# Hybrid decoder trunk on one core: the order of the input projection's blocks

## The chip, the cores and the metric

The kernel runs on one core of one Trainium2 chip. The metric is device time in microseconds of the whole program, both layers, from one launch. Times are medians of a few runs on the chip. A trace of one profiled execution shows when each instruction ran on each engine: PE (TensorE, matmuls), PEld (its weight loads), DVE (VectorE), ACT (ScalarE), POOL (GpSimd) and SP (the queue that issues the DMAs).

## What is computed

The reference runs two layers on x of shape (1, 512, 1024). Each layer has a token mixer and a channel mixer, each between two RMSNorms and added to the residual stream. Cut to what matters here:

```python
proj = h @ w_in                                   # one input projection for both groups
a_qkv, a_z, a_b, a_a, b_q, b_k, b_v = split(proj)
# group a: gated delta rule, 4 heads of 128
a_qkv = silu(causal_dwconv(a_qkv, dn_conv))       # 4 taps
aq, ak, av = split(a_qkv); aq, ak = l2norm(aq), l2norm(ak)
beta = sigmoid(a_b); g = -exp(a_log) * softplus(a_a + dt_bias)
o_a = gated_delta_rule(aq, ak, av, g, beta)       # in chunks: invert a triangle made of k, g and beta,
                                                  # then a scan over chunks that takes v, k and q
o_a = rmsnorm(o_a) * silu(a_z)
# group b: attention, 8 heads of 64, three dilations merged into one masked softmax
o_b = dilated_attention(rope(b_q), rope(b_k), b_v)
out = concat(o_a, o_b) @ w_out
```

The channel mixer is `(gelu(gate) * val) @ ffn_down` over a causal 3-tap convolution of `h @ ffn_up`.

## The kernel before

The weights are a stream of units of 128 x 1024 floats. `loader` brings them by DMA into two buffers "raw"; `splitter` turns each into a pair of reduced-precision halves (`whi` on ACT, `wlo` on POOL or DVE), for which there are four places; a place comes free when the unit's products have been issued. Each product of the projection is three matmuls (hi x hi, hi x lo, lo x hi), called a triple below.

The input projection has seven blocks of four units each: the delta rule's k, v, q and z (gate), and the attention's bq, bk and bv. The tuple ORDER (line 35) sets both the order of the weight stream (line 226) and the order in which `mixer` computes the blocks (the loop `for name in ORDER` at its end). The first three units of k are computed ahead of that loop, by `lead`, while the residual rows are still being scaled.

Two kinds of block differ in what they need:

- k, v, q, z: one unit gives one head, a tile of 128 channels by 512 tokens, in one PSUM bank of the pool "psg", which has four. `conv` takes it out of the bank into a tile "A" (times 1/rms), after which the bank is free. There are two tiles "A". The convolution that follows is one ACT instruction and three DVE instructions (line 164), and only then is the tile "A" free. For z there is no convolution. `silu` runs once for all four heads of a block and loads ACT's table for silu and the one for exp again.
- bq, bk, bv: each unit holds two of the eight row blocks of the weight for all 512 columns, and each of the four token chunks has a bank of its own, so that all four banks of "psg" are in use until the fourth unit is done. The first unit goes chunk by chunk: `order = [(c, j) for c in range(NC) for j in range(2)]`, and a bank is asked for when its chunk begins. `rope` or `v_evac` then takes the banks out through ACT.

Beside the loop run jobs of the mixer: `gates` (beta, g, and their sums, many small DVE instructions), `decays` (tile edec), `k_head`, `inverse` (the 16 x 16 blocks row by row on DVE, by way of memory) and `doubles` (the inverse of each chunk's triangle, twice as large each time, many narrow matmuls), `v_head`, `q_head`, `qk`, `scan` (over four chunks; it needs v, the inverse, and from chunk 0's output on q), `merge`, `z_head`, and `attention`, which starts when bq, bk and bv are all there and goes through eight heads, each with four scores, softmax rows in tiles "A" and "B" (two each), transposes, and two products with v. `out_rows` then multiplies by w_out, its first three row tiles in whatever order the mixer's outputs come.

The order of the instructions on every engine is fixed when the program is built. `_Sched` (line 44) keeps a clock in TensorE time and an estimate of each engine's load; jobs are generators that yield the time at which they next have something to emit, and the job of highest priority that is due emits next. The mixer's loop over ORDER has the lowest priority, so its triples fill what the jobs leave. Each engine then runs its instructions in exactly that order, and waits where an operand is late.

Of the kernel before, what the change touches and what calls it, by code (L numbers as in the profile page):

```python
# [31 lines left out]
FULL = ((0, 512),)  # L32
CM = ("k", "v", "q", "z")
TM = ("bq", "bk", "bv")
ORDER = ("k", "v", "bq", "bk", "bv", "q", "z")

C_ID, C_U, C_M, C_COS, C_SIN, C_ONE, C_BD, C_EV, C_OD = 0, 128, 256, 512, 576, 640, 641, 655, 658
C_W = 664
# [3 lines left out]


class _Sched:
    """Orders the instructions of concurrent jobs by an estimate of when their operands are ready.

    A job is a generator that emits instructions and yields the time before which it has nothing to
    emit. Times are those of the tensor engine, which advances with the products emitted."""

    def __init__(self):  # L50
        self.t = 0.0
# [26 lines left out]
        return start + cost + 0.2  # L78

    def idle(self, engs, most):  # L80
        """The first of the engines that has nothing left to do, or, after a while, the one with least."""
        end = self.t + most
        while True:
            eng = min(engs, key=lambda e: self.free[e])
            if self.free[eng] <= self.t or self.t >= end:
                return eng
            yield min(self.free[eng], end)
# [25 lines left out]
def kernel(ctx: ExitStack, tc: tile.TileContext, xT, w_ab, w_cm, w_tm, w_o, w_up, w_dn,  # L113
# [13 lines left out]

    sc = _Sched()

# [1 line left out]
    def mm(ps, lhsT, rhs, start, stop):  # L131
        n = rhs.free_size()
        if rhs.dtype == F32R:
# [42 lines left out]
        nc.vector.reciprocal(out_, a)  # L176
        return sc.op("dve", 0.07 + out_.free_size() * 6.4e-3, after)

# [1 line left out]
    BUFS = {"A": 2, "B": 2, "C": 2, "sq": 2, "acc": 1, "acc2": 1, "vh": 1, "rs": 1}  # L180
    PB = {"g": 4, "s": 3, "o": 1}

# [26 lines left out]
    one = cc[:, C_ONE:C_ONE + 1]  # L209
# [10 lines left out]

    T_EXP, T_SILU, T_GELU = "exp_and_others", "silu_and_others", "gelu_apprx_tanh_and_others"

# [1 line left out]
    wseq = []  # L224
    for l in range(DEPTH):
        for name in ORDER:
# [65 lines left out]
        mm3(ps[:, t0:t1], hi[:, k * P:(k + 1) * P], lo[:, k * P:(k + 1) * P], xh[:, t0:t1], xl[:, t0:t1],  # L292
            first, last)

# [1 line left out]
    xt = [xp.tile([P, 2, S], F32, tag=f"x{j}", name=f"xt{j}") for j in range(4)]  # L296

    def xs(m):
# [33 lines left out]
    sc.set(("vec", 0))  # L332

    def row_rstd(acc, seg, dst, tok):
        """1/rms of the columns of seg, on every partition, from the sums of squares in acc."""
        t0, t1 = seg
        c0, c1 = t0 // P, t1 // P
        ps = yield from pget("o")
        for c in range(c0, c1):
            mm(ps[:, c:c + 1], acc[:, c * P:(c + 1) * P], one, True, True)  # L340
        r = ts(tok[:, c0:c1], ps[:, c0:c1], 1.0 / D, EPS, ALU.mult, ALU.add)
        yield r
        nc.gpsimd.tensor_tensor(tok[:, c0:c1], tok[:, c0:c1], mhalf[:, c0:c1], op=ALU.pow)
        r = sc.op("pool", 0.17 + 0.15 * (c1 - c0), r)
        yield r
        for c in range(c0, c1):
            mm(ps[:, c * P:(c + 1) * P], tok[:, c:c + 1].to_broadcast([P, P]), ident, True, True)
        r = act(dst[:, t0:t1], ps[:, t0:t1], AF.Copy)
        pput("o", r)
        return r  # L350
# [7 lines left out]
        return lambda kt: (tiles[kt][:, 0], tiles[kt][:, 1])  # L358

    def scale_split(key, m, seg, hx, gain, acc2, after):  # L360
        """x * gain as an exact pair, and x^2 added to acc2."""
        t0, t1 = seg
        x = xs(m)[:, t0:t1]
        hi = hx[m][:, 0, t0:t1]
        r = act(hi, x, AF.Identity, scale=gain, after=after)
        if key != "in":
            sc.spawn(square_sum(key, m, seg, acc2), 0)
        yield r
        r = stt(hx[m][:, 1, t0:t1], x, gain, hi.bitcast(F32), ALU.mult, ALU.subtract, after=r)
        sc.set(("hx", key, m, t0), r)  # L370
        if key == "in":
            yield from sc.idle(("act",), 6.0)
            yield from square_sum(key, m, seg, acc2)
# [21 lines left out]
        return sc.flags.get(flag, 1e9) <= sc.t  # L395

    def lead(key, pss, units, rhs, seg, last, extra=None):
        """The first row tiles of a product, in whatever order their operands come."""
        n = len(units)
        left = [(i, kt) for i in range(n) for kt in range(KD)]  # L400
        if extra is not None:
            left = left[:KD] + [(n, kt) for kt in range(KD)] + left[KD:]
        while left:
            for i, kt in left:
                if ready_at(("hx", key, kt, seg[0])) and (i == n or ready_at(("wu", units[i]))):
                    break
            else:
                yield sc.t + 0.1
                continue
            mine = [k for j, k in left if j == i]  # L410
            left.remove((i, kt))
            if i == n:
                extra(kt, seg, len(mine) == KD, len(mine) == 1)
            else:
                mmk(pss[i], wunit[units[i]], kt, rhs(kt), seg, len(mine) == KD, len(mine) == 1)
                if last and len(mine) == 1:
                    wunit.pop(units[i])
                    free()
            yield

    def out_rows(key, nt, rhs, nk, post, pre, dst, wait_rhs=None, flags=None):
        """The eight row tiles of a sub-layer's result, its norm, the residual sum and, for the next
        sub-layer, x * gain as an exact pair; the last row tile and what follows by halves of the tokens."""
        yield from sc.get("acc", 1)
        acc = work("acc")
        hw, sums = {}, []
# [27 lines left out]
        if flags is not None:  # L454
# [6 lines left out]
            left = list(range(nk))  # L461
# [32 lines left out]
        if pre is not None:  # L494
            yield from sc.get("acc2", 1)
            acc2 = work("acc2")
# [101 lines left out]
        sc.put("sq", r)  # L598
        return r

# [1 line left out]
    def next_ab(l):  # L602
        wa = load_ab(l)
        yield sc.t + 4.0
# [4 lines left out]
    def mixer(l, key, hx, acc2, rs, segs):  # L609
# [115 lines left out]
            sc.set(K("gates"), r)  # L725

        def conv(kind, h, ps, ptag):
            """Row tile of k, v, q (scaled, convolved) or z (scaled), before the silu."""
            yield from sc.wait(*ready)
            m = 4 * CM.index(kind) + h  # L730
            if kind == "z":
                yield from sc.wait(*[K("x", c) for c in range(NC)])
                if not zt:
                    zt.append(sp.tile([P, 4, S], F32, tag="s6", name="zt"))
                r = tt(zt[0][:, h], ps, rs, ALU.mult)
                pput(ptag, r)
            else:
                u = yield from wget("A")
                r = tt(u, ps, rs, ALU.mult)
                pput(ptag, r)  # L740
                yield r
                dst = {"k": kT, "v": vb, "q": qraw}[kind][:, h]
                y = dst.rearrange("p c t -> p (c t)") if kind == "v" else dst
                taps = [vv[:, V_DC + 4 * m + j:V_DC + 4 * m + j + 1] for j in range(4)]
                r = conv_first(y, u, taps, None, r)
                yield r
                r = conv_rest(y, u, taps, r)
                sc.put("A", r)
            sc.set(K("cv", kind, h), r)
# [116 lines left out]
            sc.put("acc", sc.t)  # L866

        def masked(c, lv):
            """The part that joins pairs of blocks, its columns those of the even blocks."""
            s = 16 << lv  # L870
            mask = cc[:, C_M + 64 * lv:C_M + 64 * (lv + 1)].rearrange("p (a k) -> p a k", k=s)
            return tt(xiT[:, c, :, 64 * lv:64 * (lv + 1)].rearrange("p h (a k) -> p h a k", k=s),
                      am[:, c].rearrange("p h (a b k) -> p h a b k", b=2, k=s)[:, :, :, 0],
                      mask.unsqueeze(1).to_broadcast([P, 4, 64 // s, s]), ALU.mult, eng="pool")

        def expand(dst, src, s, b0, eng="dve", after=0.0):
            """Rows of diagonal blocks of s columns, put in their places in a row of 128."""
            n, nb = dst.shape[0], dst.shape[2] // s
            return tt(dst.rearrange("p h (b k) -> p h b k", b=nb),
                      src.unsqueeze(2).to_broadcast([n, 4, nb, s]),  # L880
                      bc(cc[0:n, b0:b0 + nb], s).unsqueeze(1).to_broadcast([n, 4, nb, s]), ALU.mult, eng=eng,
                      after=after)

        def doubles(c, x):
            """The inverse of a chunk's triangle from those of its diagonal blocks, twice as large each time.

            A pair of blocks has the transposed inverse [[a, -a.t.b], [0, b]]; rows keep their block's columns
            only, and what the even blocks alone need is computed for these 64 rows."""
            tmp = yield from wget("C")
            lo, up = slice(0, 64), slice(64, P)  # L890

# [382 lines left out]
        return mixt  # L1274

    def reload(xd):
        """The residual rows come back from memory once nothing else uses their place."""
        yield from sc.wait(*[(lx[0], "mt", j) for j in range(KD)])
        for j in range(4):
            xt[j] = xp.tile([P, 2, S], F32, tag=f"x{j}", name=f"xt{j}")  # L1280
# [3 lines left out]
    HG = [None]  # L1284
    lx = [0]

# [1 line left out]
    def ffn(key, hx, acc2, rs):  # L1288
        rhs = hl(hx)
        hid = [None] * 11  # L1290
# [63 lines left out]

        return lambda kt: (hid[kt // 2][:, kt % 2, 0], hid[kt // 2][:, kt % 2, 1]), wait_hid

# [1 line left out]
    def trunk():  # L1358
        nonlocal vv, rc
        key = "in"  # L1360
# [140 lines left out]
```

## Time and profile before

| | us |
|---|---|
| median of 3 runs | 1469.94 |
| lowest and highest run | 1469.23, 1472.27 |
| span of the profiled execution | 1468.8 |
| both mixers' projections, attention and delta rule (39.85 to 295.60 and 762.75 to 1025.90) | 255.8 and 263.2 |

The page gives the span of the profiled execution from its first to its last instruction; the time around it isn't on the page, and the median of the timed runs lies 1.1 us above the span. Timeline rows give start, duration, engine, line, operation, what is written and read, shape, and a count where neighbours were merged; in brackets, how long the engine was idle before and what ended that. A row of a window table gives busy time and count of each engine, then the granted TensorE clock as a share of full speed, DMA share and GB/s.

### The profile page before, as it was taken

Reading aid. Unit: us, or ns where it says so; the run is one execution under the profiler, and the core shown is the slowest. Engines: PE = TensorE matmul, PEld = TensorE weight load, DVE = VectorE, ACT = ScalarE, POOL = GpSimd, SP = SyncE. Lnnn points to the kernel's source line nnn. Section 1 sums busy time; section 2 is a strip of 40 time slices with the busy share of each in tenths; the row PEclk is TensorE's granted clock in tenths of the full one; section 3 lists DMA queues with packets and bytes.
Section 4 is the critical chain, followed back from the end, with each engine's and each line's share of the span. In section 5 each row is a group of like instructions: output and inputs, shape, how many; then the busy total and the mean of one; then the engine's idle time right before and its main releaser. Section 6 shows DMA issues by size and latency. Waiting matters only on the chain.

```text
span 1468.8 us, 18826 instructions
## 1 busy us (share of the span) xinstructions
PE 1400.0 (95%) x7174; PEld 1155.5 (79%) x7174; DVE 941.8 (64%) x1497; ACT 610.3 (42%) x992; POOL 603.1 (41%) x365
## 2 busy tenths in 40 slices
PE   8999999998999999899999999999989999998996
PEld 5778766887888888788887877668878888887886
DVE  4885576757788877611479654668487887886113
ACT  4553456544543444322345423565255344433220
POOL 4244255315454444433343521553164444543332
PEclk9999999999999999999999987999989999999998
DMA  5233111041323322333232330110413332233331
GB/s 193 72 98 104 32 44 44 1 149 53 101 86 101 100 87 87 105 93 100 76 126 86 104 85 15 44 44 16 143 44 101 101 100 86 87 101 104 93 90 58
DMA packets 48698, 123.15 MB, mean 84 GB/s; under 512 B 15584, under 2 KB 18400, under 8 KB 48608
## 3 DMA queue, kind: packets, MB, share of 16 engines
q1 hardware_dynamic: 48608, 121.95, 26.7%
q8 instruction: 57, 0.93, 0.3%
q14 instruction: 33, 0.27, 0.1%
HBM read 115.11 MB, written 6.82 MB: 83 GB/s over the span
## 4 chain that ended last, share of the span: by engine, by line
PE 63%; DVE 25%; ACT 7%; issue 4%; DMA 0%; SPq 0%; POOL 0%; ACTq 0%; DVEq 0%
PE psg L137 49%; DVE B L164 12%; PE pss L137 9%; ACT B L146 3%; PE pso L137 2%; DVE kT L164 2%; DVE C L150 2%; ACT hid L146 1%; DVE xt L150 1%; PE pss L142 1%; DVE A L150 1%; PE psg L142 1%; DVE hx L164 1%; DVE zt L150 1%; ACT whi L146 1%
## 5 line engine op out<-in xcount | busy, mean ns | idle before, releaser
L137 PE MATMUL psg<-hx,whi 128*128 128x512 f32 (+1 forms) x2080 | 630.1, 386 | 0.9 <-DVE C L157 0.8
L150 POOL TENSOR_TENSOR wlo<-raw,whi 128x1024 fp32r<-128x1024 f32 (+1 forms) x159 | 394.5, 2490 | 557.9 <-ACT whi L146 535.8
L137 PEld LDWEIGHTS psg<-hx,whi 128*128 128x128 f32 x2080 | 378.8, 189 | 78.6 <-issue 4.9
L137 PE MATMUL psg<-hx,wlo 128*128 128x512 f32 (+1 forms) x1040 | 396.9, 382 | 0.0
L146 ACT ACTIVATE whi<-raw 128x1024 fp32r<-128x1024 f32 (+1 forms) x208 | 215.5, 1036 | 274.3 <-PE psg L137 212.5
L164 DVE SCALAR_TENSOR_TENSOR B<-A,vv,B 128x510 f32<-128x510 f32 (+1 forms) x176 | 275.3, 1565 | 76.9 <-ACT B L146 73.8
L137 PE MATMUL psg<-hid,whi 128*128 128x512 f32 (+1 forms) x792 | 224.8, 369 | 8.8 <-ACT hid L146 8.7
L137 PEld LDWEIGHTS psg<-hx,wlo 128*128 128x128 f32 x1040 | 196.6, 189 | 38.2
L137 PEld LDWEIGHTS psg<-hid,whi 128*128 128x128 f32 x792 | 144.5, 190 | 34.9 <-ACT hid L146 9.6
L137 PE MATMUL psg<-hid,wlo 128*128 128x512 f32 (+1 forms) x396 | 145.7, 368 | 0.0
L150 DVE TENSOR_TENSOR wlo<-raw,whi 128x1024 fp32r<-128x1024 f32 (+1 forms) x49 | 66.1, 1353 | 102.0 <-ACT whi L146 96.0
L137 PE MATMUL psg<-whi,hx 128*128 128x512 f32 x384 | 125.4, 408 | 0.3 <-DVE A L150 0.3
L146 ACT ACTIVATE hid<-C 128x512 fp32r<-128x512 f32 x44 | 27.7, 630 | 179.4 <-DVE C L150 179.4
L137 PE MATMUL pss<-hx,whi 128*128 128x256 f32 (+1 forms) x336 | 80.8, 330 | 20.9 <-DVE hx L164 18.5
L150 POOL TENSOR_TENSOR acc<-acc,sq 128x256 f32<-128x256 f32 (+1 forms) x65 | 67.7, 1041 | 75.1 <-ACT sq L146 72.0
L137 PEld LDWEIGHTS psg<-hid,wlo 128*128 128x128 f32 x396 | 75.3, 190 | 12.2
L137 PEld LDWEIGHTS pss<-hx,whi 128*128 128x128 f32 x336 | 61.0, 212 | 28.8 <-DVE hx L164 22.2
L146 ACT ACTIVATE B<-A,vv 128x512 f32<-128x512 f32 x88 | 71.0, 809 | 25.8 <-DVE A L150 24.5
L137 PEld LDWEIGHTS psg<-whi,hx 128*128 128x128 f32 x384 | 70.4, 192 | 13.7 <-DVE A L150 0.8
L137 PE MATMUL psg<-wlo,hx 128*128 128x512 f32 x192 | 76.4, 398 | 0.0
L150 DVE TENSOR_TENSOR A<-psg,rs 128x512 f32<-128x512 f32 x100 | 68.2, 684 | 2.0 <-POOL A L157 1.6
L137 PE MATMUL psg<-bT,bT 64*128 64x512 f32 (+3 forms) x128 | 48.4, 478 | 6.9 <-DVE nm L1151 4.2
(226 smaller groups left out, 1674.5 us busy)
## 6 DMA issues: line engine op xcount, KB each, us to landing
raw<-in_w_up_dram SPq DMA_DIRECT2D x88, 512.0 KB, 3.5
raw<-in_w_cm_dram SPq DMA_DIRECT2D x32, 512.0 KB, 3.6
raw<-in_w_dn_dram SPq DMA_DIRECT2D x32, 512.0 KB, 3.5
raw<-in_w_tm_dram SPq DMA_DIRECT2D x24, 512.0 KB, 3.5
raw<-in_w_o_dram SPq DMA_DIRECT2D x16, 512.0 KB, 3.6
raw<-in_w_dn_dram SPq DMA_DIRECT2D x16, 384.0 KB, 3.1
xt<-in_xT_dram SPq DMA_DIRECT2D x7, 512.0 KB, 6.9
scr_a<-am SPq DMA_DIRECT2D x8, 256.0 KB, 2.9
```

The costliest lines, as they stand in the source:

```text
L137: pe.matmul(ps, lhsT, rhs, start=start, stop=stop)
L142: pe.transpose(dst[:, i * P:(i + 1) * P], s, ident)
L146: nc.scalar.activation(out_, in_, func, **kw)
L150: (nc.vector if eng == "dve" else nc.gpsimd).tensor_tensor(out_, a, b, op=op)
L164: nc.vector.scalar_tensor_tensor(out_, a, s, b, op0=op0, op1=op1)
```

## The change

ORDER puts v behind the three attention blocks. Comments and docstrings were removed as well; the rest is the same code. The weight units are the same and are split in the same way, in the new order.

```diff
 CM = ("k", "v", "q", "z")
 TM = ("bq", "bk", "bv")
-ORDER = ("k", "v", "bq", "bk", "bv", "q", "z")
+ORDER = ("k", "bq", "bk", "bv", "v", "q", "z")
...
     for l in range(DEPTH):
         for name in ORDER:
...
         for name in ORDER:
             if name in CM:
```

## The prediction

> **What bounds the kernel now.** I read the page's first lines, then the busy time of each engine by stage, the list of TensorE's waits in the first mixer, and then the timelines of PE, DVE and POOL around the place where the order changes. First the page, with the rows of the weight loads from its list of DMA issues.
>
> ```profile
> span 1468.8 us, 18826 instructions
> PE 1400.0 (95%) x7174; PEld 1155.5 (79%) x7174; DVE 941.8 (64%) x1497; ACT 610.3 (42%) x992; POOL 603.1 (41%) x365
> ...
> raw<-in_w_cm_dram SPq DMA_DIRECT2D x32, 512.0 KB, 3.6
> ...
> raw<-in_w_tm_dram SPq DMA_DIRECT2D x24, 512.0 KB, 3.5
> ```
>
> PE is busy 95% of the span; no other engine is near it. The change alters no instruction and no count, only where the value units stand, so only time in which PE waits, or runs at a reduced clock, can change. The table by stage shows how much of that there is. In layer 0, 39.85 is where the last key unit ends and 165.70 where the attention projections end; 295.60 is where the output projection starts. In layer 1 the same places are 762.75, 896.27 and 1025.90; 145.40 and 866.20 are where the doubling of the inverse starts. Columns: stretch, PE, PEld, DVE, ACT, POOL (left out where it is zero), granted clock, DMA.
>
> ```profile
> 39.85:69.75 29.90, 27.46 (x141) 22.54 (x140) 25.93 (x47) 14.54 (x23) 9.84 (x4) 1.00 0.22 71
> ...
> 145.40:165.70 20.30, 19.95 (x166) 15.96 (x165) 8.73 (x28) 6.54 (x12) 2.40 (x1) 0.92 0.18 61
> 165.70:295.60 129.90, 123.32 (x713) 94.14 (x712) 91.03 (x239) 71.33 (x160) 59.27 (x42) 0.96 0.10 32
> ...
> 866.20:896.27 30.07, 28.81 (x167) 23.36 (x165) 9.71 (x28) 6.54 (x12) 2.36 (x1) 0.58 0.15 51
> 896.27:1025.90 129.63, 123.05 (x714) 94.06 (x712) 90.50 (x238) 71.64 (x160) 59.29 (x42) 0.97 0.11 33
> ```
>
> The stretch with attention, queries, gate and scan (165.70 to 295.60) already has PE busy 123.32 of 129.90 us: the query and gate units fill what attention leaves. Starting attention earlier therefore finds little idle PE time to fill. The 20.30 us of doubling in layer 0 take 30.07 us in layer 1, for the same work, at a clock of 0.58 instead of 0.92: 9.8 us that only the clock explains. The waits of PE between 33 and 296 us (total, times, longest), and behind them the first row of the same list for 755 to 1026 us:
>
> ```profile
> PE pso L137 <- DVE edec L150: 2.9, 2, 2.3
> PE psg L137 <- DVE nm L1151: 2.1, 1, 2.1
> PE pss L142 <- DVE kd L150: 1.7, 1, 1.7
> PE pso L137 <- DVE pt1l L150: 1.5, 1, 1.5
> PE psg L142 <- DVE pt L150: 1.4, 1, 1.4
> PE psg L137 <- DVE pt1l L150: 1.4, 1, 1.4
> ...
> PE psg L137 <- DVE A L150: 0.3, 1, 0.3
> ```
>
> ```profile
> PE pso L137 <- DVE edec L150: 3.0, 1, 3.0
> ```
>
> Two kinds: about 4.9 us early (edec, kd, A), while the key and value convolutions crowd DVE, and about 6.4 us in the attention stretch (nm, pt1l, pt). None names ACT.
>
> **The change part by part: the fourth bank.** A value, query or gate unit needs one PSUM bank of the pool "psg" (four banks). An attention projection needs all four at once: `pt` collects one per token chunk, and its first weight unit goes chunk by chunk, two row blocks each. Directly behind the keys, one bank is still held by the fourth key tile, k3, until its convolution takes it. The timelines of PE, DVE and POOL there:
>
> ```profile
> 39.62 0.39 PE L137 MATMUL psg<-hx,wlo 128*128 128x512 f32 x1
> 39.85 0.62 PE L137 MATMUL psg<-hx,whi 128*128 128x512 f32 x2
> ...
> 40.55 0.62 PE L137 MATMUL psg<-hx,whi 128*128 128x512 f32 x2
> ...
> 42.00 0.41 PE L668 MATMUL pso<-cc,C 16*128 16x16 f32 x4
> ...
> 57.05 0.39 PE L137 MATMUL psg<-hx,wlo 128*128 128x512 f32 x1
> 57.56 0.70 PE L137 MATMUL psg<-hx,whi 128*128 128x512 f32 x2
> ```
>
> ```profile
> 34.29 0.67 DVE L172 COPY C<-psg 16x512 f32<-16x512 f32 x1
> ...
> 47.10 8.83 DVE L164 SCALAR_TENSOR_TENSOR kT<-A,vv,kT 128x509 f32<-128x509 f32 x6
> 55.85 0.68 DVE L150 TENSOR_TENSOR A<-pss,rs 128x512 f32<-128x512 f32 x1
> ...
> 56.74 0.68 DVE L150 TENSOR_TENSOR A<-psg,rs 128x512 f32<-128x512 f32 x1
> 57.34 6.67 DVE L164 SCALAR_TENSOR_TENSOR kT<-A,vv,kT 128x509 f32<-128x509 f32 x6
> ...
> 68.08 4.55 DVE L164 SCALAR_TENSOR_TENSOR vb<-A,vv,vb 128x509 f32<-128x509 f32 x6 [0.34 <-ACT vb L146]
> ```
>
> ```profile
> 47.05 2.39 POOL L150 TENSOR_TENSOR wlo<-raw,whi 128x1024 fp32r<-128x1024 f32 x1 [3.70 <-ACT whi L146]
> 52.99 2.39 POOL L150 TENSOR_TENSOR wlo<-raw,whi 128x1024 fp32r<-128x1024 f32 x1 [3.55 <-DMA raw<-in_w_tm_dram]
> ```
>
> The small-gate bank is free from 34.96 (34.29 + 0.67). k3's is freed only at 57.42 (56.74 + 0.68): its evacuation needs a tile "A", of which there are two, and those are held by k0 and k1 until the six products from 47.10 are done. Before, three value units of about 5.6 us stood in that gap (8 triples of 0.70, from the starts 39.85 and 40.55), and the fourth starts at 57.56, right behind the evacuation; the bank was just not missed. After, PE does three chunks (six triples, 4.2 us, and the 0.41 us of L668) and stops at 44.4. The group from 47.10 ends at 47.10 + 8.83 = 55.93 today. DVE's gate chain up to 47.10 doesn't depend on the order. The six products then take 4.55 us, as the value ones at 68.08 did, not 8.83: the two POOL splits beside them cost the rest, (8.83 - 4.55)/2 = 2.1 each, and those weights are split later or earlier because no unit is freed meanwhile. So 51.7, and from there to k3's evacuation as before, 57.42 - 55.93 = 1.5: 53.2. PE waits from 44.4 to 53.2, less some 0.5 for the four g sums, which still go out in between: **8.2 us** (12.5 if the splits stay where they are; 4.4 if the key products go ahead of the gate chain).
>
> Layer 1, the same views:
>
> ```profile
> 762.75 0.62 PE L137 MATMUL psg<-hx,whi 128*128 128x512 f32 x2
> ```
>
> ```profile
> 766.46 8.71 DVE L164 SCALAR_TENSOR_TENSOR kT<-A,vv,kT 128x509 f32<-128x509 f32 x6
> ...
> 775.97 0.68 DVE L150 TENSOR_TENSOR A<-psg,rs 128x512 f32<-128x512 f32 x1
> ```
>
> Three chunks end at 762.75 + 4.2 = 766.9. One of two POOL splits remains, since its weights land late: 766.46 + 6.6 + 1.5 = 774.6. **7.2 us** after 0.5 for the g sums (5 to 9.4). Behind the blocked PE nothing else is queued that is ready: decays and key transposes need the key convolutions. The weight stream is 512 KB a unit at 3.5 to 3.6 us in either order, so SP's queue sees the same loads with two names exchanged.
>
> **The clock after the waits.** Rows in steps of 4 us around two waits of today, 2.1 us at 248 and 3.0 us at 782:
>
> ```profile
> 248.00:252.00 4.00, 1.89 (x3) 0.50 (x2) 3.50 (x8) 1.19 (x4) 4.00 (x3) 0.70 0.28 72
> 252.00:256.00 4.00, 4.00 (x14) 3.47 (x14) 0.83 (x4) 0.57 (x1) 2.79 (x3) 0.50 0.15 59
> ...
> 784.00:788.00 4.00, 2.91 (x15) 2.91 (x16) 2.14 (x4) 3.97 (x5) 0.00 (x0) 0.68 0.03 10
> 788.00:792.00 4.00, 4.00 (x24) 3.64 (x23) 3.86 (x7) 3.94 (x7) 0.00 (x0) 0.89 0.00 0
> ```
>
> The first loses 4 x (0.30 + 0.50) = 3.2 us of full clock, the second 4 x (0.32 + 0.11) = 1.7. For two waits I take 2 each, **+4** (0 to 6.4).
>
> **What the early crowd loses.** With the value convolutions gone from the first 40 us, DVE reaches the decays sooner. The early waits are 4.9 us in layer 0, and 3.0 and the 1.7 of clock in layer 1: 9.6. The key convolutions stay, so I take two thirds, **-6.4** (0 to -9.6).
>
> **What the values bring to attention.** Four value convolutions (4 x 2.3 us of DVE) and their silu now lie among softmax rows and doublings. The query convolutions do so today, beside waits of 1.4 us for pt and pt1l. I take 2 us a layer, **+4** (0, if the heads have slack, to 13, if both layers repeat the 2.1 + 1.4 us waits with a 3.2 us clock loss). The silu adds ACT time only, and no PE wait names ACT.
>
> **The doubling.** It moves beside attention and value units. In the old order its second half already runs beside the first heads. Layer 1, after 896.27:
>
> ```profile
> 900.00:916.00 16.00, 16.00 (x124) 11.38 (x124) 10.12 (x43) 7.74 (x23) 4.34 (x5) 1.00 0.11 34
> ```
>
> The clock is 1.00 there. I take the 9.8 us of layer 1 as gone, **-9.8** (0 to -9.8).
>
> **The end of the mixer.** Attention starts some 34 us earlier (the four value units, 22 us, and the 20.3 us of doubling no longer stand ahead of it, the 8.2 us wait does) and ends before the scan; queries stay sixth of seven, so the scan starts no earlier. The chain from queries to output projection is covered by the gate units (32 triples, 22 us), the scan's own products and the attention half of the output projection. I take 0 (-3 to +8).
>
> Sum: 8.2 + 7.2 + 4 - 6.4 + 4 - 9.8 = **+7.2 us** on the profiled execution (span 1468.8). The median lies 1.1 above that span, so I add the sum to it: 1469.9 + 7.2 = **1477 us**.
>
> **Rivals.** First, the clock stretch stays, in one layer or the other. For it: both layers ran the same doubling, and only one was throttled. Then +17.0: 1487. [...]
>
> Second, DVE becomes the bound while attention, doubling and eight convolutions lie together: 13 in place of 4, so +16: 1486. DVE is busy 91.03 of 129.90 in the attention stretch today, without doubling and values; that leaves room, against it.
>
> Third, on the other side: attention without the scan beside it loses its waits. Price: the 6.4 us of waits in each layer and the clock (4% of 129.9 and 3% of 129.6, 9 us) make 22. If two thirds of it go, and the values add nothing: 7.2 - 4 - 14.7 = -11.5: 1458. It decides from 7.2 - 4 + 2.9 = 6.1 us, 28% of the 22: from there the kernel is faster by over 0.2%.
>
> Fourth, the fourth bank isn't missed, because the key convolutions are ordered earlier: the waits shrink to their lower ends, 9.4, with no clock loss. That gives 9.4 - 6.4 + 4 - 9.8 = -2.8: 1467, about no change.
>
> **How the numbers follow.** Forecast 0.42, clock rival 0.17, DVE rival 0.09, faster attention 0.18, no missing bank 0.14. 0.2% (2.9 us) is about what a measurement of this kernel can tell from no change. The forecast's own spread (1470 to 1484) puts a tenth of it inside 0.2%. Slower 0.38 + 0.17 + 0.09 = 0.64, same 0.04 + 0.11 = 0.15, faster 0.18 + 0.03 = 0.21. The range for 8 in 10 runs from 1460, inside the third rival, to 1490, above the first two; the slower cases alone span 1473 to 1490.
>
> **What would show it.** In the profile after: PE idle for some 8 us from about 44 and 767 us, released by DVE's "A" (its row rises from 0.3 us to about 15 in total), a reduced clock behind it, fewer waits for edec and kd, first scores near 135 us rather than behind 165.70, and the doubling at a clock near 1.00 in both layers. I am wrong at the first step if PE runs through from 40 to 57 us; at the third if its waits for pt1l, pt and nm fall well below 6 us a layer; at the doubling if a stretch of half clock remains.

## The result, and the profile after

The kernel with the new order takes 1486.7 us (median of four runs, 1485.1 to 1495.8) against 1470.7 us, a ratio of 1.0126 with a 95% interval of 1.0104 to 1.0149. It is slower by 16 us; the forecast was 1477, with 1460 to 1490 as its range. A run more than 1.5% above the fastest run of its kernel counts as slow: the ratios here leave such runs out, and they are not quotients of the medians. The profiled execution of after is the one of 1486.01 us.

First its page: the span and the busy time of the engines.

```profile
span 1484.2 us, 18809 instructions
...
PE 1410.9 (95%) x7174; PEld 1166.6 (79%) x7174; DVE 928.0 (63%) x1503; ACT 621.4 (42%) x998; POOL 579.1 (39%) x357
```

PE is as busy as before in share, and 11 us busier in time, with the same 7174 products: the products themselves take longer (1410.9 us against 1400.0, a mean of 196.7 ns against 195.1). The two layers show where. The products that read `hid` (the down projections) start first in layer 0's FFN and last in layer 1's; their summary in the view of that tile, of before and then of after, gives two marks: the first start and the last.

```profile
L137 PE MATMUL psg<-hid,whi x792: 277/389/795, 595.8 to 1454.2; 128*128 128x512 f32 x154, 128*128 128x256 f32 x44
```

```profile
L137 PE MATMUL psg<-hid,whi x792: 277/389/796, 608.2 to 1469.6; 128*128 128x512 f32 x154, 128*128 128x256 f32 x44
```

Up to the first mark, which holds mixer 0, after is 12.4 us later. From there to the second, which holds mixer 1, it takes 861.4 us against 858.4, 3.0 more. The new order is in both layers; what differs is what the old order lost in them.

PE's waits in after's first mixer (33 to 320 us), largest first:

```profile
PE psg L137 <- DVE A L150: 4.9, 1, 4.9
PE pso L137 <- DVE dn_g L164: 2.6, 1, 2.6
PE psg L137 <- ACT hx L146: 2.3, 1, 2.3
PE pss L142 <- DVE B L150: 1.4, 2, 1.0
PE psg L137 <- DVE hx L150: 1.2, 1, 1.2
PE pss L142 <- DVE A L150: 0.9, 2, 0.7
PE pso L137 <- DVE pt L150: 0.8, 1, 0.8
...
PE pso L137 <- DVE pt1l L150: 0.3, 1, 0.3
```

Against the list of before: edec and kd are gone, A and dn_g (the fourth bank) are new, and so is hx, at the start of the output projection. The attention waits (nm, pt1l, pt) have shrunk from 6.4 to 1.1 us, which the forecast had the other way round. Layer 1 (755 to 1050 us) has its bank wait first and the same waits for hx at its end. It has none for dn_g, and one more, of 1.5 us, for hx at line 164:

```profile
PE psg L137 <- DVE A L150: 7.3, 1, 7.3
PE psg L137 <- ACT hx L146: 2.3, 1, 2.3
```

**The fourth bank** is where the forecast put it. The timelines of PE and of DVE in layer 0:

```profile
44.05 0.40 PE L137 MATMUL psg<-wlo,hx 128*128 128x512 f32 x1
47.06 1.01 PE L137 MATMUL pso<-dn_g,cc 128*128 128x16 f32 x4 [2.62 <-DVE dn_g L164]
52.92 1.22 PE L137 MATMUL psg<-whi,hx 128*128 128x512 f32 x2 [4.85 <-DVE A L150]
```

```profile
46.84 4.54 DVE L164 SCALAR_TENSOR_TENSOR kT<-A,vv,kT 128x509 f32<-128x509 f32 x6
...
52.19 0.68 DVE L150 TENSOR_TENSOR A<-psg,rs 128x512 f32<-128x512 f32 x1
```

The six key products take 4.54 us with no split of POOL's beside them (POOL idles from 43.1 to 56.65 us; with two splits beside them they took 8.83 in before), and k3's bank is free at 52.19 + 0.68 = 52.87, where 53.2 was forecast. PE stands still for 2.62 + 4.85 = 7.5 us.

**The doubling** is where the time went. Its stretch in both layers of after, and the edges of the reduced clock in layer 0 (columns as in the prediction: PE, PEld, DVE, ACT, POOL, clock, DMA):

```profile
134.50:174.40 39.90, 39.90 (x271) 31.83 (x270) 19.70 (x73) 11.73 (x33) 3.55 (x4) 0.66 0.06 18
868.50:908.00 39.50, 39.50 (x267) 31.45 (x267) 19.39 (x72) 11.58 (x32) 3.55 (x4) 0.65 0.06 16
```

```profile
137.00:138.00 1.00, 1.00 (x12) 1.00 (x11) 0.97 (x4) 0.97 (x4) 0.00 (x0) 1.00 0.78 307
138.00:165.00 27.00, 27.00 (x148) 21.09 (x147) 10.22 (x40) 7.34 (x20) 2.75 (x3) 0.52 0.02 5
165.00:166.00 1.00, 1.00 (x10) 0.88 (x10) 0.00 (x0) 0.34 (x2) 0.00 (x0) 0.50 0.00 0
166.00:167.00 1.00, 1.00 (x17) 0.93 (x15) 0.73 (x4) 0.00 (x0) 0.00 (x0) 0.94 0.00 0
```

The clock falls to half with PE busy in every row (27.00 of the 27.00 us from 138, at 0.52), so no wait goes with it, and it stays down for 27 us (27.3 by the clock changes that the trace records). In the old order layer 0 ran its doubling at 0.92 and layer 1 at 0.58; now both are like layer 1, at 0.66 and 0.65. What stands between the narrow products differs. The wide products in the 20.30 us from 145.40 of before, and in the 41 us from 134 of after:

```profile
L137 PE MATMUL psg<-whi,hx 128*128 128x512 f32 x14 | 5.5, 475 | 0.0
...
L137 PE MATMUL psg<-wlo,hx 128*128 128x512 f32 x8 | 3.4, 423 | 0.0
```

```profile
L137 PE MATMUL psg<-hx,whi 128*128 128x512 f32 x8 | 3.8, 562 | 0.0
...
L137 PE MATMUL psg<-hx,wlo 128*128 128x512 f32 x4 | 2.0, 510 | 0.0
```

These are some seven triples in 20 us before, and four in 41 us after: behind the attention projections the scores and transposes of the first heads take the places that the last projection's triples had.

**The end of the mixer** has a wait that before did not have. PE and DVE at the start of the output projection of layer 0:

```profile
312.26 0.50 PE L137 MATMUL psg<-hx,whi 128*128 128x512 f32 x1 [2.31 <-ACT hx L146]
314.01 0.80 PE L137 MATMUL psg<-hx,whi 128*128 128x512 f32 x1 [1.25 <-DVE hx L150]
```

```profile
310.85 2.50 DVE L150 TENSOR_TENSOR zt<-zt,vb 128x512 f32<-128x512 f32 x4 [1.78 <-ACT vb L146]
313.27 2.49 DVE L150 TENSOR_TENSOR hx<-zt,hx 128x512 fp32r<-128x512 f32 x4
```

The last part of the delta rule (`zt`) ends last, with nothing wide left beside it. A reason shows in the summary of ACT's silu of the queries, in before and then in after:

```profile
L146 ACT ACTIVATE qraw<-qraw x1: 1913/1913/1913, 232.0 to 232.0; 128x2048 f32<-128x2048 f32 x1
```

```profile
L146 ACT ACTIVATE qraw<-qraw x1: 1919/1919/1919, 266.5 to 266.5; 128x2048 f32<-128x2048 f32 x1
```

The queries are sixth of seven in both orders, but attention, a job of higher priority, now goes ahead of the values and queries, and puts the queries back by 34.5 us, about as far as it starts earlier itself (its first score at 135.5 us, against 168.9).

**The account.** The clock changes that the traces record are all between 1.00 and 0.50 (the records of before and after hold no other value, and no 2 us row of eleven other traces lies below 0.50), so (1 - clock) x 2 x length, summed over rows, is the time at half clock, and length minus PE's busy time is its idle time. Summed over rows of 2 us up to the second mark, before has 56.4 us idle and 81.9 at half clock, after 60.9 and 116.0. Over the profiled executions of twelve kernels (all below but the one that holds attention for the queries and the one without doubling), length = 1366 + idle + 0.40 x half clock fits each within 5 us. The 0.40 has a standard error of 0.05, so it is not sharply told from 0.5; the kernel that holds attention for the queries, left out of the fit, lies within 1 us of it. A second figure agrees: the same doubling took 20.30 us in layer 0 of before and 30.07 in layer 1, 9.8 us more with 23.9 us more of half clock, which is 0.41, or 0.37 without the 0.9 us that PE is idle more. So of the 15.4 us between the two second marks, 4.5 are idle time and 34.1 x 0.40 = 13.6 are clock, with 2.7 the other way that the fit leaves. The errors of the fit are not small beside the single terms.

That also fits the runs of one kernel. Of 58 runs of the kernel before, made beside the experiments, 5 lie at 1458 to 1462 us with a mean clock of 0.974 to 0.976, 48 at 1467 to 1473 with 0.965 to 0.970, and 5 at 1477 to 1482 with 0.958 to 0.963. The levels lie some 11 us apart: 27.3 x 0.40 = 10.9, about one such stretch more or less. The mean clocks of the levels, 0.975, 0.967 and 0.960, say nearly the same: 0.0075 x 2 x 1470 is 22 us of half clock from one to the next. No trace shows one kernel at two levels.

### The profile page after: what moved, and what is told of

Same layout as the page of the kernel before. It is cut to its first block, busy times and chain, and to the rows that moved or that the text cites. A ratio compares the mean times of both kernels' runs of the same rounds, so it can differ in the third digit from the quotient of the medians.

```text
span 1484.2 us, 18809 instructions
## 1 busy us (share of the span) xinstructions
PE 1410.9 (95%) x7174; PEld 1166.6 (79%) x7174; DVE 928.0 (63%) x1503; ACT 621.4 (42%) x998; POOL 579.1 (39%) x357
## 5 line engine op out<-in xcount | busy, mean ns | idle before, releaser
L150 POOL TENSOR_TENSOR wlo<-raw,whi 128x1024 fp32r<-128x1024 f32 (+1 forms) x153 | 378.0, 2480 | 533.1 <-ACT whi L146 510.3
L150 DVE TENSOR_TENSOR wlo<-raw,whi 128x1024 fp32r<-128x1024 f32 (+1 forms) x55 | 73.3, 1336 | 116.7 <-ACT whi L146 116.6
L137 PEld LDWEIGHTS psg<-whi,hx 128*128 128x128 f32 x384 | 71.7, 193 | 26.1 <-DVE A L150 12.4
L137 PEld LDWEIGHTS psg<-hid,wlo 128*128 128x128 f32 x396 | 75.2, 190 | 12.2
L157 POOL TENSOR_SCALAR A<-A,den 128x128 f32<-128x128 f32 (+1 forms) x30 | 29.1, 969 | 122.0 <-DVE den L176 74.2
```

Of the source, the lines that this page charges most:

```text
L137: pe.matmul(ps, lhsT, rhs, start=start, stop=stop)
L150: (nc.vector if eng == "dve" else nc.gpsimd).tensor_tensor(out_, a, b, op=op)
L157: e.tensor_scalar(out_, a, s1, None, op0=op0)
```

## The experiments

All ratios are to the kernel before, run on the same chip beside them. Idle and half clock are those of the profiled execution, up to its last `hid` product.

| kernel | median us | ratio, 95% interval | idle | half clock |
|---|---|---|---|---|
| before | 1470.7 | | 56.4 | 81.9 |
| after | 1486.7 | 1.0126, 1.0104 to 1.0149 | 60.9 | 116.0 |
| after_k3_spare | 1493.4 | 1.0128, 1.0071 to 1.0185 | 54.5 | 122.9 |
| before_k3_spare | 1467.5 | 0.9995, 0.9972 to 1.0017 | 51.8 | 75.2 |
| after_attention_held | 1610.6 | 1.0947, 1.0899 to 1.0996 | 125.0 | 259.5 |
| after_values_by_four | 1492.2 | 1.0135, 1.0099 to 1.0171 | 69.6 | 105.7 |
| after_held_for_values | 1517.7 | 1.0332, 1.0273 to 1.0390 | 81.8 | 112.5 |
| after_held_values_spare | 1501.6 | 1.0211, 1.0148 to 1.0275 | 68.5 | 133.0 |
| new_order_layer0_only | 1483.1 | 1.0073, 1.0032 to 1.0113 | 56.9 | 92.1 |
| new_order_layer1_only | 1472.7 | 1.0045, 1.0012 to 1.0079 | 58.5 | 99.0 |
| after_scores_behind_doubling | 1490.1 | 1.0157, 1.0100 to 1.0215 | 64.1 | 99.0 |
| before_bv_by_four | 1459.3 | 0.9926, 0.9904 to 0.9948 | 47.2 | 81.9 |
| before_spare_bv_by_four | 1473.8 | 1.0026, 0.9993 to 1.0059 | 49.8 | 129.8 |
| after_without_doubling | 1441.5 | 0.9799, 0.9779 to 0.9819 | 72.1 | 71.7 |

### The fourth bank taken away

```diff
 def conv(kind, h, ps, ptag):
-    u = yield from wget("A")
+    spare = kind == "k" and h == 3
+    if spare:
+        u = bv[:, 0]
+    else:
+        u = yield from wget("A")
...
-    sc.put("A", r)
+    if not spare:
+        sc.put("A", r)
```

> The new order, with one part changed: the fourth key tile's evacuation goes to a slice of the bv tile, which is idle until the third attention projection ends, and no longer waits for a tile A. Theory (the fourth bank is a wait of its own): the waits for A (4.9 us in layer 0, 7.3 in layer 1) and for dn_g (2.6) go, and with them the reduced clock behind them (10.2 us at half clock in layer 0, 6.8 in layer 1, worth 5.1 and 3.4): some 14.8 + 5 to 8.5, so 20 to 23 us less than 1486.7, about 1464 to 1468. Rival (the convolutions of DVE are merely late everywhere): PE is stopped a little later by kd and edec instead, as in the kernel before, and half of it comes back: about 1476. Second rival (the end of each mixer is set by the chain of the delta rule, not by PE's work): the early gain turns into a longer wait at the output projection, and the time stays within 4 us of 1486.

The theory's waits went, and the time did not. PE runs through where it stood still, at full clock; and later, behind the projections of layer 1, the clock is down for 44 of 62 us:

```profile
39.00:60.00 21.00, 21.00 (x102) 17.29 (x101) 16.74 (x35) 6.21 (x11) 7.18 (x3) 1.00 0.32 97
...
867.90:930.00 62.10, 61.69 (x324) 45.22 (x323) 30.23 (x97) 19.74 (x52) 12.41 (x9) 0.59 0.06 18
```

Idle time fell by 6.4 us in all and not by 14.8, since PE meets other waits earlier (3.5 for A at the key transposes in layer 0, 2.3 for the spare tile itself in layer 1), and half clock rose by 6.9. The waits for hx at the output projection stayed at 2.3 and 1.2 us. So the bank's wait is real and removable, but it is not by itself what makes the new order slower: without it the order is as far behind (1.0128), with another draw of the clock.

> The old order with the same spare place for the fourth key tile, as a control. Theory: the bank isn't missed there, since the value units need one bank each, so the time stays at 1470.7 within 3 us. Rival (the A tiles themselves hold up the first 40 us, by way of edec and kd): the early waits (4.9 us in layer 0, 3.0 in layer 1, and the clock behind them) shrink and it is 4 to 8 us faster, 1463 to 1467.

No difference, as the theory had it: the old order does not miss the bank. Its idle time is 4.6 us less, though the wait for edec is longer (4.3 and 5.3 us), and the ratio cannot be told from 1. The waits for nm, pt1l and pt are gone here too, and at the output projection PE waits for hx (1.5 + 1.3 us in each layer), there for attention's outputs: such waits are not peculiar to the new order.

### Attention held back

One line ahead of the first score; the flags waited for are the query convolutions, the value convolutions, or the finished doublings:

```diff
 def attention():
     yield from sc.wait(*[K("bv", c) for c in range(NC)])
+    yield from sc.wait(*[K("cv", "q", h) for h in range(NH)])
```

> The new order, with attention held until the query convolutions are done, as it would stand if only the projections were early. Theory (the tail comes from attention going ahead of the queries, whose silu starts at 266.5 us where it was 232.0): the queries come back to about 235, the waits for hx at the start of the output projection (2.3 + 1.2 us a layer, and 6.8 us of half clock behind them) go, and attention again fills the scan: 5 to 7 us a layer less from the tail, but the waits of attention (nm, pt, pt1l) come back with 4 to 9 us a layer, so the time is 1478 to 1490 and the trace shows the tail gone. Rival (the tail comes from PE being late by the fourth bank's wait alone): the waits at the output projection stay as they are. On the clock of the doubling: if the first scores beside the doubling set it, the 27.3 us of half clock go in both layers; if the narrow products of the doubling alone set it, it stays.

Far off, and for a plain reason that the expectation missed: with attention last, the value and query units are used up ahead of it. The queries did come early (213.8), but the last heads then ran alone, idle for 21 of 69 us and at half clock throughout:

```profile
308.00:377.00 69.00, 47.90 (x122) 28.22 (x123) 19.58 (x60) 19.62 (x50) 14.55 (x13) 0.51 0.00 0
```

The doubling, with no score beside it, is at half clock for 10.2 us in layer 0 and 23.9 in layer 1: neither side of that question. In layer 1 that is so although 128x512 products take 19.0 of the 26 us from 946 (12.6 + 6.4), so there wide products beside the doubling did not bring the clock back.

> The new order, with attention held only until the value convolutions are done, so that it has the query and gate units beside it as in the kernel before. Theory (the end of the mixer waits because attention, which goes ahead of the projections, put the queries back by 34 us): the queries' silu comes back from 266.5 to about 235 us, PE's waits for hx at the output projection (2.3 + 1.2 us a layer, with 6.8 us of half clock) go, the attention waits of the kernel before (nm, pt1l, pt, some 6 us a layer) come back; the fourth bank's waits stay. In time that is about even: 1478 to 1490. Rival (the waits at the output projection come from something else, such as the order of the last units): they stay, and the time goes to 1490 to 1500.

The time is 1517.7, above both numbers. The queries came back to 232.4 as expected, and the delta rule's first output with them (from 313.3 to 293.3 us), so their delay does put the delta rule back. But the waits at the output projection stayed, so the first half of the theory fell in part: the wait is not the queries' as such. Here the attention chain is the one that ends last, with the same lack of wide work beside it. PE at 310 us:

```profile
313.77 2.07 PE L137 MATMUL psg<-bT,bT 64*128 64x512 f32 x2 [0.77 <-DVE nm L1152]
316.83 0.44 PE L142 MATMUL psg<-cc,A 128*128 128x128 f32 x1 [0.99 <-DVE den L176]
318.12 0.66 PE L142 MATMUL psg<-cc,B 128*128 128x128 f32 x2 [0.84 <-DVE pt L150]
```

Its first score came at 192.8, against 168.9 in before and 135.5 in after. Two chains, attention and the delta rule, must end together for PE to run on into the output projection; in before they nearly did. The doubling, now without scores, is at half clock for 10.2 us in each layer.

> The same hold, and the fourth key tile in the idle bv slice as well, so that both known costs of the new order are away. Theory (fourth bank and late queries are all that the order costs beside the clock): the time is that of the kernel before with the same spare place, 1467.5, within 8 us as the doubling's clock falls. Rival (the doubling beside value units instead of the last attention projection costs by itself): 1478 or more, with doubling at half clock in both layers for 27 us or more.

1501.6: within the rival's number, but not with its clock, which was to be down for 27 us or more in both doublings. The fourth bank's waits are gone (idle 13 us less than with the hold alone) and half clock is 20 us more: 20.5 us on end in the doubling of layer 0, and in layer 1 27.3 beside the last heads, from 1045, where the doubling has only 10.2. Why the clock fell in the one place or the other was not tracked.

> The new order, with attention held only until the last doubling of the inverse is done, so that value units, not scores, lie beside the doubling. [...] The first scores start near 155, earlier than the 168.9 of the kernel before, so the end of attention is no later than there, and the time falls by 5 to 15 us to 1472 to 1482. [...] Second rival (holding attention leaves it without wide work at its end, as the two other holds showed with 1517.7 and 1610.6): the half clock of the doubling shrinks and yet the time is 1490 or above, with waits for nm, den and pt near 310 us.

The stretch of each layer, from the first doubling to the first score:

```profile
137.90:172.00 34.10, 33.85 (x276) 26.47 (x275) 20.46 (x55) 8.81 (x18) 4.50 (x2) 0.95 0.13 38
868.60:911.60 43.00, 42.75 (x277) 32.69 (x276) 21.72 (x58) 8.84 (x18) 4.72 (x2) 0.72 0.13 38
```

With value triples in place of scores, layer 0's half clock falls to 3.4 us and layer 1's only to 23.9: nearly the two values that the old order has with the last projection's triples there (3.4 and 27.3), where 3.4 to 13.7 was expected of each. So beside single triples among the doublings (17 in layer 0's stretch) the clock was 0.95 in one layer and 0.72 in the other; the runs with the new order in one layer, below, show that scores do not settle it either. The first scores came at 172 and not at 155, as the doublings last until 169. The time is 1490.1, the second rival's, but not with its waits: at the output projection PE waits for hx (2.0 + 1.3 us), and for nm only 0.9 us in the whole mixer. By idle time and half clock the profiled execution should be 3.6 us shorter than that of after, and it is 4.3 longer at the second mark (1473.9 against 1469.6); where that went stays open.

### How many wide products on end

```diff
 for kt in range(KD):
     mmk(ps, u, kt, rhs(kt), FULL[0], kt == 0, kt == KD - 1)
-    yield
+    if name != "v" or kt % 4 == 3:
+        yield
```

> The new order, with the value units issued four triples at a time, 2.8 us of 128x512 products on end, where one triple stood between groups of narrow products. [...] Rival (a stretch once at half clock lasts 27.3 us whatever stands in it): the stretches of 27.3 us stay, and the time stays within 4 us of 1486.

```profile
138.50:175.00 36.50, 35.34 (x210) 27.60 (x209) 20.20 (x62) 11.50 (x27) 7.52 (x5) 0.72 0.11 35
873.30:912.00 38.70, 37.53 (x211) 28.90 (x210) 20.28 (x62) 11.50 (x27) 7.53 (x5) 0.69 0.11 33
```

The half clock of these stretches fell from 27.3 us to 20.5 and 23.9, in two pieces each: less than was expected (3.4 or 6.8 us left in each), and against the rival, since it isn't one fixed length. In exchange the attention waits grew (pt1l 5.5 us in each layer), the waits for hx at the output projection went, with the queries' silu at 247.1, and the time rose to 1492.2, where 1470 to 1480 was expected.

In the old order, the third attention projection by four (in its first unit seven and one, in its last three and one by turns):

```diff
 for c, j in order:
...
-    yield
+    if name != "bv" or c == NC - 1 or ui == 3 and c % 2:
+        yield
```

> The old order, with the units of the third attention projection, which lie beside the first half of the doubling, issued four triples at a time (2.8 us of wide products on end). [...] Second rival (the clock in the doubling is chance): the half clock there neither shrinks in both layers nor grows in both.

1459.3, ratio 0.9926: faster than both kernels, and by more than expected (1462 to 1466), but not through less half clock, which is what was expected. Layer 1's stretch did shrink, to 10.2 us, yet layer 0 has 10.2 there and two of 6.8 behind it, and the sum is 81.9 us as before:

```profile
165.00:225.00 60.00, 58.84 (x375) 45.83 (x375) 36.21 (x113) 22.88 (x60) 16.96 (x14) 0.81 0.07 19
886.80:940.00 53.20, 52.55 (x374) 40.51 (x373) 36.24 (x113) 22.76 (x60) 15.91 (x13) 0.90 0.07 21
```

The gain of the profiled execution is idle time, 9.2 of 10.3 us up to the last mark. PE's waits from 150 to 320 us, where before has 2.1 for nm, 2.9 for pt1l and 1.4 for pt:

```profile
PE psg L137 <- DVE hx L150: 1.4, 1, 1.4
PE psg L142 <- DVE den L176: 1.2, 1, 1.2
PE psg L137 <- DVE nm L1151: 0.6, 1, 0.6
```

> The old order with both changes that went the right way: the third attention projection issued four triples at a time (1459.3 alone) and the fourth key tile in the idle bv slice (1467.5 alone, 1469.3 to 1470.1 without). Theory (the two act on different stretches and add): 1455 to 1458. Rival (the spare place only moves the waits for edec, 4.3 and 5.3 us there, and the clock decides): 1458 to 1463.

The two do not add. The idle time is low again (49.8), but both doublings fell to half clock (30.7 and 34.1 us on end) and the half clock rose by 48 us:

```profile
160.00:192.00 32.00, 31.47 (x170) 24.67 (x169) 12.44 (x46) 8.55 (x22) 2.77 (x3) 0.52 0.00 1
891.00:926.00 35.00, 34.47 (x180) 27.31 (x179) 13.10 (x48) 9.58 (x25) 2.96 (x4) 0.51 0.00 1
```

### One layer at a time

```diff
-ORDER = ("k", "bq", "bk", "bv", "v", "q", "z")
+ORDER = (("k", "bq", "bk", "bv", "v", "q", "z"),
+         ("k", "v", "bq", "bk", "bv", "q", "z"))
...
-for name in ORDER:
+for name in ORDER[l]:
```

> The new order in layer 0, the old one in layer 1. Theory (the account by layer from the two profiled executions, 12.4 us in layer 0 and 3.0 in layer 1, holds, because layer 1 had its half clock in the doubling already): 1470.5 + 12.4, so 1480 to 1486. Rival (that split is luck of two executions, and each layer costs the same): 1476 to 1479.

> The old order in layer 0, the new one in layer 1. Theory (the new order itself costs some 3 us in a layer, by the waits of PE; the other 10 us of layer 0 were its doubling falling to half clock, which layer 1's did in the old order already): 1469.3 + 3, so 1470 to 1475, and the half clock in the doubling is as in the kernel before, short in layer 0 and some 27 us in layer 1. Rival (the new order costs the same 7 to 8 us in each layer, since the cost of layer 0 alone came out at 13.8): 1476 to 1484.

The medians are 13.8 and 2.4 us above before, inside the theory's bounds and together the 16 us of after. The intervals of the ratios (1.0032 to 1.0113, 1.0012 to 1.0079) overlap, so the medians point to the split but don't prove it. Taken from the ratios it is less sharp: 0.0073 and 0.0045 of 1470 us are 10.7 and 6.6 us, the second between the theory's 3 and the rival's 7 to 8. The traces show more, because in both the profiled execution was not the usual one. With the new order in layer 0 (1473.5 us, the lowest level of its ten runs; the other seven lie at 1482 or above, two beside it below 1476), the doubling of that layer kept most of its clock:

```profile
134.40:174.00 39.60, 39.60 (x310) 31.64 (x310) 24.61 (x92) 17.38 (x48) 8.67 (x8) 0.91 0.07 20
```

There the first mark stands at 599.1, 3.3 us behind before's and not 12.4: that is about what the new order costs a layer when the doubling keeps most of its clock (6.8 us of half clock in it, against 3.4 in before). With the new order in layer 1 alone, one of the higher runs was profiled (1479.7), and there layer 0, in the old order, has the stretch that before was spared:

```profile
145.90:178.00 32.10, 31.29 (x175) 25.52 (x175) 9.42 (x28) 8.86 (x16) 3.45 (x2) 0.57 0.09 31
865.00:904.00 39.00, 39.00 (x273) 31.03 (x274) 20.37 (x75) 12.08 (x35) 3.56 (x4) 0.69 0.05 17
```

So neither order fixes the clock in layer 0's doubling: it was 0.66 in one execution and 0.91 in the other in the new order, 0.92 and 0.57 in the old. Layer 1's was at half clock for 27.3, 27.3, 27.3 and 23.9 us in the four (before, after, new order in layer 0 alone, in layer 1 alone). That the new order draws half clock more often in layer 0 is read from the levels of the runs (seven of ten at the higher ones), not from traces.

### The doubling left out

```diff
 def doubles(c, x):
+    r = ts(xiT[:, c], am[:, c], 0.0, None, ALU.mult)
+    sc.put("cpt", r)
+    sc.set(K("x", c), r)
+    yield r
+    return
```

> The new order without the products of the doubling, and without the small operations between them: the tile of the inverse is filled with zeros by one operation a chunk, so the delta rule adds nothing. What is measured is the clock behind the third attention projection, where the first scores and the value units now stand alone. In the kernel after, the doubling's seven groups are busy for 28.4 of the 39.9 us from 134.5 (8.6 + 4.0 + 3.6 + 3.6 + 3.5 + 3.0 + 2.1), at a mean clock of 0.66. Theory (the narrow products of the doubling hold the clock down): no half clock beyond 3.4 us between 134 and 175 or between 868 and 909, and the time falls by those 28 us and the clock of the rest, some 31 us a layer, to 1420 to 1432. Rival (the first scores and transposes hold it down as well without them): 13 us or more of half clock in each layer behind the projections, and the time falls by less, to 1436 to 1455.

```profile
134.00:144.00 10.00, 10.00 (x41) 6.82 (x40) 6.51 (x16) 4.63 (x12) 2.87 (x2) 1.00 0.45 114
...
154.00:164.00 10.00, 10.00 (x51) 7.34 (x50) 6.97 (x20) 4.55 (x13) 7.18 (x5) 1.00 0.16 52
...
878.00:888.00 10.00, 9.43 (x46) 6.62 (x45) 7.05 (x21) 5.13 (x14) 4.75 (x5) 1.00 0.15 54
```

There is no half clock in these stretches in either layer: beside scores and value triples alone the clock was 1.00, and with the doubling's narrow products, in after, 0.66 and 0.65. Leaving them out also draws the wide products together: 33 triples in the 40 us from 134, where after has four in 41. The run shows what the mix does, not the narrow products apart from the lack of wide ones. (Farther on in attention a stretch of 3.4 us is left in each layer, at 204 and 914.) The spread of the runs shrinks too, to 1440.6 to 1441.8. The clock is as the theory had it; the time, 1441.5, is in the rival's range. It fell by 45 us, not by the 55 to 67 of the theory: waits that the doubling had covered are open now (nm 2.1, vb 1.7 and POOL's B 1.9 us in layer 0).

## Why the prediction was right in sign and short in size

- **The fourth bank**, 8.2 and 7.2 us: right. Measured 2.6 + 4.9 = 7.5 and 7.3, released at the forecast place.
- **The clock after the waits**, +4: right in kind, short in size. It is 10.2 us at half clock in layer 0 and 6.8 in layer 1, at 0.40 some 6.8 us.
- **What the early crowd loses**, -6.4: right in kind, too large. edec and kd are gone (2.9 + 1.7 and 3.0), and DVE's B and A at the transposes took part of their place (1.4 + 0.9 a layer): about -3.4, and 1.4 of clock in layer 1.
- **What the values bring to attention**, +4: wrong in sign. The waits fell from 6.4 us to 1.1 in a layer, about -10, and 10.2 and 6.8 us of half clock behind them went too, -6.8: -17 in all. The third rival's mechanism was real; its time was not, since the next two used it up.
- **The end of the mixer**, 0 (-3 to +8): wrong. The step said that queries, sixth of seven, start the scan no earlier, and did not ask whether they start it later. They do, by 34.5 us, because whatever starts earlier at a higher priority delays the units behind it. The end has 3.5 us of waits and 6.8 of half clock in each layer, some 12.5 in all. That the late queries put the delta rule back is shown (after_held_for_values brought both back); that they alone cost the 12.5 is not, as there the wait moved to attention's end.
- **The doubling**, -9.8: the step that failed, and the largest. Layer 1's stretch remained at 27.3 us and layer 0's grew from 3.4 to 27.3: 23.9 x 0.40 = +9.6 where -9.8 was forecast. The prediction took the second half of the doubling, beside the first heads at a clock of 1.00, as the pattern for the whole; but that row has 4 wide triples to 83 narrow products of the doubling, where after's stretch has 4 to 224 (64 + 16 + 32 + 32 + 32 + 32 + 16, from the groups of its lines). That this share sets the clock was the author's estimate; the same stretch of layer 0 ran at 0.91 with the new order in layer 0 alone. The clock rival, at 1487 with a chance of 0.17, named the right stretch and had too low a chance. Its wording, that the stretch "stays in one layer or the other", was still mild: it came in both. That its time was right too is partly luck: it took the doubling at 0, where it cost 9.6 us, and its other terms were off by about as much the other way.

Summed: the doubling was off by +19.4 and the mixer's end by +12.5, attention and values by -21, the three smaller terms by +3.8 together, which is +14.7. Idle time outside the steps fell (1.9 us in the first 20 us of the kernel, 1.7 of waits for xi), and 2.7 is what the fit of the clock's price leaves; that makes 8.4, and 15.4 - 7.2 = 8.2 is what the forecast missed up to the last mark. So it is luck that the sum missed by no more: two terms were off by 32 us together and one by 21 the other way.

The traces show where the clock changes. Single stretches of half clock measure 3.41 us, the others whole multiples of it (6.8, 10.2, 13.7, 23.9, 27.3 and more); in before and after only the one behind the program's last products is not (13.0 and 12.8 us). In the clock records of before and after all half-clock stretches begin whole multiples of 3.4133 us apart, to within 2 ns; in the 2 us rows of eleven other traces (all but the one without doubling), to within 0.05 us. In the doubling of after no idle time goes with the half clock: PE is busy for 27.00 of the 27.00 us from 138.

What stays open is why equal instructions draw the one clock or the other. One thing differs between executions: where this grid of 3.413 us lies. Reckoned back from the stretches, its first point behind the first instruction comes after 0.39 us in the trace of before, 2.29 in after, 0.08 with the new order in layer 0 alone and 3.01 with it in layer 1 alone. So the same products lie elsewhere on the grid; that this decides the draw was not tested. The runs show half clock in the mix with the narrow products (0.66 and 0.65 in after) and none in the same stretches without them; what keeps the clock up was not shown.

## What to carry to other kernels

Wide products are cover for PE's waits: where the last heads ran without them, PE was idle for 21 of 69 us (after_attention_held). Whether they also hold its clock up beside narrow products these runs leave open: with some seven triples in the doubling of before it was 0.92 in one layer and 0.58 in the other, and in the stretch of layer 0 that has four in after it was 0.66 there and 0.91 with the new order in layer 0 alone. Count them in each stretch before an order moves them, and read the clock of such a stretch as a draw, not as its property. A job of higher priority that starts earlier delays all that stands behind it: ask which of two chains then ends last, and what is left beside it. When a fix removes its wait and the time stays, add up idle time and half-clock time by stage before blaming the fix.

## What the runs showed of the hardware

- A PE that the profile shows busy without a gap ran at half clock for 27 us (after, 138 to 165: busy 27.00, clock 0.52), with products of 16 to 64 columns as the bulk of its work (106 of the 148); without those products, in the same place and with 33 wide triples for four, the clock was 1.00 (after_without_doubling).
- Half clock cost 0.40 us for each us spent in it, by the twelve executions (standard error 0.05), and 0.37 to 0.41 by the two doublings of before.
- The clock changed on a grid of 3.413 us in thirteen traces; it is fixed within an execution and lay elsewhere in another (0.39 us behind the first instruction in before, 2.29 in after).
- One stretch of 27.3 us is worth an estimated 11 us of 1470 (27.3 x 0.40). The layer with the old order had it in one trace (27.3 us, new order in layer 1 alone) and not in another (3.4, before), and the levels of the 58 runs of before fit one stretch more or less.
